# Weight splits ordered behind the scaling of every pair

## The chip, the cores and the metric

The program runs on one core of one Trainium2 chip. The metric is the device time of the whole program in microseconds (us), lower is better; it is given as the median of several executions of the same build.

## What is computed

A two-layer decoder trunk on 256 tokens of width 1024, all in float32, with a memory of 256 tokens beside it. Each layer is half a feed-forward net, a mixer, and another half of a feed-forward net. In the first layer the mixer is a gated short convolution beside a cross-attention to the memory; in the second it is latent attention (MLA), whose shared keys and values come from the residual stream after the first layer, beside another cross-attention.

```python
def swiglu(h, w13, w2):                    # D_FF = 2816
    gate, up = jnp.split(h @ w13, 2, axis=-1)
    return (jax.nn.silu(gate) * up) @ w2

# four times in the trunk (two layers, two halves each):
x = x + 0.5 * swiglu(rms_norm(x, g), w13, w2)
```

## The kernel before

Everything is kept transposed: 128 partitions hold a slice of the model's width, 256 tokens lie along the row. TensorE works on pairs of a high and a low part of each number, so that float32 accuracy survives: a product is two matmuls where one operand is an activation (`mm2`, lines 196 and 197: high weights against 128x512, then low weights against 128x256) and three where both are split (`mm3`, lines 190 to 192).

**Weights.** All weight tiles (128x1024, 512 KB) stand in one list in the order of use, a `Stream` called `W`. SyncE (SP) loads them one after the other into six raw buffers (`wraw`). A tile is *split* into a high part, by a cast on ScalarE (ACT, L69), and a low part, by a subtraction on VectorE (DVE, L70), both into one of eight `whl` buffers. `W.get(key)` hands out the next tile; `W.pump()` issues loads up to 9 tiles and splits up to 5 tiles beyond the last one handed out. While it does so, `issue_after(ins)` for each instruction in `W.hold` puts what it issues behind that instruction in the order of that instruction's engine. The instruction held on is a DVE one, so it is the L70 subtractions that are ordered; casts and loads have no such edge, but a load needs a raw buffer that the subtraction six tiles earlier has freed.

**Stages.** Four half feed-forward stages, with the conv mixer after the first and MLA after the third. A half feed-forward stage goes over 22 *pairs* j = 0 to 21 of a 128-wide slice of gate and one of up. For pair j, `begin(j)` issues 32 matmuls into two PSUM banks (`pg`, `pm`), copies the low half of each bank out on ACT (L483) and adds it to the high half on DVE (L484). `make(j)` scales the result by the row norm R (DVE, L488: the instruction called `evac`), pumps, applies silu (ACT, L494), multiplies gate by up (DVE, L497) and splits the product into the activation tile g (ACT L182, DVE L183). `accumulate` runs two pairs behind and adds g against a tile of w2 (one tile serves two pairs) in 8 matmuls into four banks `acc`. In the first and the third stage some pairs begin with an *insert*, a step of other work: in the first (to about 84 us of the span) the memory's norm and its key and value projections (`spare`, 48 `mm3` matmuls each); in the third (about 504 to 725 us) the shared K/V of MLA: its projection from three tiles at pair 4 (L839 copies it out, L848 to L853 norm it, L860 scales the rotary part), transposes of the latent at pair 6 (L868) and of the rotary part (L881, which waits for the rotary arithmetic on GpSimd, POOL, L800 to L863).

**Order.** A scheduler places the instructions of each engine at build time, by what depends on what and in the order of issue in the text; on the chip each engine then works through its list in that order.

Of the kernel before, what the change touches and what calls it, by code (L numbers as in the profile page):

```python
# [108 lines left out]
def trunk(ctx: ExitStack, tc: tile.TileContext, a, out):  # L109
# [57 lines left out]
    def bank():  # L167
        return pg.tile([P, 2, T], F32, name="pg")

    def mbank():  # L170
        return pm.tile([P, 2, T], F32, name="pm")

    def abank(q):
        return pa.tile([P, 2, T], F32, name=f"acc{q}")

    def keep(i, shape=(P, 2, T), dt=F32R):

        return res.tile(list(shape), dt, name=f"g{i}")
# [10 lines left out]
    def mm3(o, lhs, rhs, start, stop):  # L189
        nc.tensor.matmul(o, lhs[0], rhs[0], start=start, stop=False, skip_group_check=True)  # L190
        nc.tensor.matmul(o, lhs[0], rhs[1], start=False, stop=False, skip_group_check=True)  # L191
        nc.tensor.matmul(o, lhs[1], rhs[0], start=False, stop=stop, skip_group_check=True)  # L192

    def mm2(o, lhs, x, start, stop):

        nc.tensor.matmul(o, lhs[0], x, start=start, stop=False, skip_group_check=True)  # L196
        nc.tensor.matmul(o[:, 0, :], lhs[1], x[:, 0, :], start=False, stop=stop, skip_group_check=True)  # L197
# [54 lines left out]
    W = Stream(tc, wraw, whl, "w", units, 9, 5)  # L252
# [4 lines left out]
    def new_stage():  # L257
        xs["hl"] = res.tile([P, KD, 2, T], F32R, name="xs")
        xs["tot"] = w1.tile([P, T], F32, name="tot")
# [38 lines left out]
    def r_row(s, mk=lambda i: mbank()):  # L298

        rc = xs["rc"] = r_col(s, "x", ps=mk(2))  # L300
        yield
        dg = w1.tile([P, 2, P], F32, name="dg")
        ps = mk(3)
        for t in range(2):
            nc.vector.tensor_scalar(out=dg[:, t, :], in0=ident, scalar1=rc[:, t:t + 1], scalar2=None, op0=ALU.mult)
        for t in range(2):
            nc.tensor.matmul(ps[:, 0, t * P:(t + 1) * P], ones, dg[:, t, :], start=(t == 0), stop=(t == 1),
                             skip_group_check=True)
        R = w1.tile([P, T], F32, name="R")
        nc.vector.tensor_copy(out=R, in_=ps[:, 0, :])  # L310
        yield R


    def evict(d, b, factor, norm):

        xk = xT[:, d, :]
        for h in range(1 if norm is None and d == KD - 1 else 2):
            nc.vector.scalar_tensor_tensor(out=xk, in0=b[:, h, :], scalar=factor, in1=xk, op0=ALU.mult, op1=ALU.add)
        if norm is None:
            nc.sync.dma_start(out=out[:, d * T:(d + 1) * T], in_=xk)  # L320
            return
        if d >= 6:
            feed_square(d)
        feed_split(d, norm)
        if d < 6:
            feed_square(d)

    def accumulate(gen, total_n, bkey, factor, norm):


        acc = [None] * 4
        gs = []
        for n in range(total_n):
            gs.append(gen(n))
            if n % 2 == 0:
                w = W.get(bkey + (n // 2,))
            W.pump()
            for d in range(4):
                if n == 0:
                    acc[d] = abank(d)  # L340
                o = n % 2 * 512 + d * P
                mm2(acc[d], (w[:, 0, o:o + P], w[:, 1, o:o + P]), gs[n], n == 0, n == total_n - 1)
        if norm is not None:
            new_stage()
        for d in range(4):
            evict(d, acc[d], factor, norm)
        for d in range(4, KD):
            b = mbank() if d % 2 else bank()
            for n in range(total_n):
                i, o = divmod((d - 4) * total_n + n, 8)  # L350
                if o == 0:
                    w = W.get(bkey + (total_n // 2 + i,))
                    W.pump()
                ww = (w[:, 0, o * P:(o + 1) * P], w[:, 1, o * P:(o + 1) * P])
                if norm is None and d == KD - 1:
                    mm3(b[:, 0, :], ww, (gs[n][:, 0, :], gs[n][:, 1, :]), n == 0, n == total_n - 1)
                else:
                    mm2(b, ww, gs[n], n == 0, n == total_n - 1)
            evict(d, b, factor, norm)
# [61 lines left out]
    def pairs(keyf, row, bank=bank1, late=False, head=None):  # L421

        st = {}

        def go(n):
            if n == 0 and head is not None:
                st["p0"], st["p1"] = bank(), bank()
                for q in range(4):
                    head(q)
                    c = q // 2  # L430
                    for j in range(2):
                        ps = st[f"p{j}"]
                        w = heads[2 * c + j]
                        for k in (2 * q, 2 * q + 1):
                            for s in range(2):
                                o = k % 4 * 256 + s * P
                                mm2(ps[s], (w[:, 0, o:o + P], w[:, 1, o:o + P]), xs["hl"][:, k], k == 0, k == KD - 1)
                        if q == 3 and j == 0:
                            next(row)
                for c in range(2):  # L440
                    for j in range(2):
                        W.get(keyf(j, c))
                return st["p0"]
            if n == 0:
                st["p0"], st["p1"] = bank(), bank()
                proj(keyf(0, 0), st["p0"], 0)
                proj(keyf(1, 0), st["p1"], 0, lambda: next(row))
                proj(keyf(0, 1), st["p0"], 1)
                if not late:
                    st["R"] = next(row)  # L450
                    proj(keyf(1, 1), st["p1"], 1)
                return st["p0"]
            if n == 1:
                if late:
                    if head is None:
                        proj(keyf(1, 1), st["p1"], 1)
                    st["R"] = next(row)
                return st["p1"]
            ps = bank()
            for c in range(2):  # L460
                proj(keyf(n, c), ps, c)
            return ps
        return go, st

    def rb(R):
        return R.rearrange("p (o t) -> p o t", o=1).broadcast_to([P, 2, T])

    def ffn(l, f, inserts, next_norm, head=None):
        go, st = pairs(lambda j, c: ("w13", l, f, j, c), r_row(xs["tot"], abank), lambda: (bank(), mbank()),
                       True, head)  # L470
        ready = {}
        if head is None:
            with tc.issue_after(xs["fed"][0].ins):
                W.ahead(W.used + 7, W.used + 5)

        def begin(j):
            if j in inserts:
                next(inserts[j], None)
            ps = go(j)
            e = ev.tile([P, 2, T], F32, name="ev")  # L480
            part = wk.tile([P, 2, T], F32, name="sq")
            for s in range(2):
                nc.scalar.copy(out=part[:, s, :], in_=ps[s][:, 1, :])  # L483
                nc.vector.tensor_tensor(out=e[:, s, :], in0=ps[s][:, 0, :], in1=part[:, s, :], op=ALU.add)  # L484
            return e

        def make(j, e):
            evac = nc.vector.tensor_tensor(out=e, in0=e, in1=rb(st["R"]), op=ALU.mult)  # L488
            if j < 2:
                W.hold = (evac.ins,)  # L490
            if j:
                W.pump()
            sl = wk.tile([P, T], F32, name="silu")
            act = nc.scalar.activation(out=sl, in_=e[:, 0, :], func=AF.Silu)  # L494
            xs["evac"], xs["act"] = evac.ins, act.ins
            gg = wk.tile([P, T], F32, name="gg")
            nc.vector.tensor_tensor(out=gg, in0=sl, in1=e[:, 1, :], op=ALU.mult)  # L497
            g = keep(j)
            split(gg, None, g[:, 0, :], g[:, 1, :])
            return g  # L500

        def gen(n):
            if n == 0:
                e0 = begin(0)
                e1 = begin(1)
                ready[0] = make(0, e0)
                ready[1] = make(1, e1)
            if n + 2 < NJ:
                ready[n + 2] = make(n + 2, begin(n + 2))
            return ready.pop(n)  # L510

        accumulate(gen, NJ, ("w2", l, f), 0.5, next_norm)


# [168 lines left out]
    def conv_mixer(next_norm):  # L683
# [60 lines left out]
        def gen(n):  # L744
# [11 lines left out]
            return ready.pop(k)  # L756

        accumulate(gen, 8, ("wo", 0), 1.0, next_norm)


# [550 lines left out]
```

## Time and profile before

| | us |
|---|---|
| median of 3 executions | 977.25 (976.89 to 978.62) |
| the profiled execution, its own time | 978.48 |
| its span in the trace | 976.6 |
| PE busy in the span | 959.2 |
| DVE busy | 741.1 |
| ACT busy | 558.4 |

The span is what the trace covers; the 1.9 us between it and the execution's own time lie around it. "Busy" of PE means that some matmul was in flight. A wait is the time in which an engine stood still, put down to the instruction that released it.

### The profile page before, as it was taken

Reading aid. Unit: us, or ns where it says so; the run is one execution under the profiler, and the core shown is the slowest. Engines: PE = TensorE matmul, PEld = TensorE weight load, DVE = VectorE, ACT = ScalarE, POOL = GpSimd, SP = SyncE. Lnnn points to the kernel's source line nnn. Section 1 sums busy time; section 2 is a strip of 40 time slices with the busy share of each in tenths; the row PEclk is TensorE's granted clock in tenths of the full one; section 3 lists DMA queues with packets and bytes.
Section 4 is the critical chain, followed back from the end, with each engine's and each line's share of the span. In section 5 each row is a group of like instructions: output and inputs, shape, how many; then the busy total and the mean of one; then the engine's idle time right before and its main releaser. Section 6 shows DMA issues by size and latency. Waiting matters only on the chain.

```text
span 976.6 us, 15585 instructions
## 1 busy us (share of the span) xinstructions
PE 959.2 (98%) x5856; PEld 849.7 (87%) x5856; DVE 741.1 (76%) x1412; ACT 558.4 (57%) x961; POOL 22.4 (2%) x47
## 2 busy tenths in 40 slices
PE   8889999999999999999999899999999999999998
PEld 7788898889998888888888788888897998888887
DVE  7978777784988797777858888677778679777771
ACT  7746555554555465555645666556556766555550
POOL 3100000000000000000000200000010000000000
PEclk9989999999999999999999999999999999999999
DMA  8676555551654386666535656554544318756540
GB/s 306 198 249 223 194 186 174 183 197 59 224 187 154 115 281 202 191 199 188 171 117 186 231 175 192 183 194 159 183 139 130 92 45 280 232 194 190 177 133 20
DMA packets 50332, 174.11 MB, mean 178 GB/s; under 512 B 5840, under 2 KB 7376, under 8 KB 50256
## 3 DMA queue, kind: packets, MB, share of 16 engines
q1 hardware_dynamic: 49680, 172.45, 53.4%
q8 instruction: 46, 0.75, 0.3%
q10 hardware_dynamic: 576, 0.66, 0.2%
q14 instruction: 30, 0.25, 0.1%
HBM read 172.04 MB, written 1.05 MB: 177 GB/s over the span
## 4 chain that ended last, share of the span: by engine, by line
PE 91%; DVE 5%; DMA 1%; ACT 1%; issue 1%; POOL 1%; ACTq 0%; POOLq 0%; SPq 0%; DVEq 0%
PE pg L196 20%; PE pm L196 20%; PE pg L197 10%; PE pm L197 10%; PE acc L196 8%; PE acc L197 4%; PE pg L190 2%; PE pg L192 2%; PE pg L191 2%; DVE whl L70 2%; PE pm L190 1%; PE pm L192 1%; PE pm L191 1%; PE acc L190 1%; PE acc L192 1%; PE acc L191 1%
## 5 line engine op out<-in xcount | busy, mean ns | idle before, releaser
L70 DVE TENSOR_TENSOR whl<-wraw,whl 128x1024 fp32r<-128x1024 f32 (+3 forms) x330 | 390.4, 1198 | 94.3 <-ACT whl L69 94.2
L69 ACT CAST whl<-wraw 128x1024 fp32r<-128x1024 f32 (+3 forms) x330 | 338.1, 1029 | 176.2 <-PE pm L197 81.7
L196 PE MATMUL pg<-xs,whl 128*128 128x512 f32 x704 | 255.4, 396 | 1.5 <-ACT whl L69 1.5
L196 PE MATMUL pm<-xs,whl 128*128 128x512 f32 x704 | 254.5, 395 | 0.0
L197 PE MATMUL pg<-xs,whl 128*128 128x256 f32 x704 | 197.4, 280 | 0.8 <-DVE whl L70 0.8
L197 PE MATMUL pm<-xs,whl 128*128 128x256 f32 x704 | 196.3, 279 | 0.0
L196 PEld LDWEIGHTS pg<-xs,whl 128*128 128x128 f32 x704 | 132.1, 188 | 31.5 <-ACT whl L69 2.0
L196 PEld LDWEIGHTS pm<-xs,whl 128*128 128x128 f32 x704 | 132.0, 188 | 30.4 <-ACT g L839 0.2
L196 PE MATMUL acc<-g,whl 128*128 128x512 f32 x384 | 138.8, 397 | 2.6 <-DVE g L183 2.5
L197 PEld LDWEIGHTS pg<-xs,whl 128*128 128x128 f32 x704 | 132.6, 188 | 3.8 <-DVE whl L70 3.6
L197 PEld LDWEIGHTS pm<-xs,whl 128*128 128x128 f32 x704 | 132.6, 188 | 0.3
L197 PE MATMUL acc<-g,whl 128*128 128x256 f32 x384 | 107.1, 279 | 0.0
L196 PEld LDWEIGHTS acc<-g,whl 128*128 128x128 f32 x384 | 72.0, 188 | 21.0 <-DVE g L183 4.5
L197 PEld LDWEIGHTS acc<-g,whl 128*128 128x128 f32 x384 | 72.3, 188 | 0.0
L483 ACT COPY sq<-pm 128x256 f32<-128x256 f32 x88 | 32.8, 372 | 68.8 <-PE pm L197 68.8
L196 PE MATMUL pg<-g,whl 128*128 128x512 f32 x192 | 68.2, 397 | 0.0
L182 ACT CAST g<-gg 128x256 fp32r<-128x256 f32 x94 | 38.0, 404 | 45.4 <-DVE gg L497 41.2
L488 DVE TENSOR_TENSOR ev<-ev,R 128x512 f32<-128x512 f32 x88 | 62.0, 708 | 2.2
L196 PE MATMUL pm<-g,whl 128*128 128x512 f32 x170 | 60.3, 398 | 0.0
L484 DVE TENSOR_TENSOR ev<-pm,sq 128x256 f32<-128x256 f32 x88 | 37.3, 424 | 27.8 <-ACT sq L483 27.7
L183 DVE TENSOR_TENSOR g<-gg,g 128x256 fp32r<-128x256 f32 x94 | 39.7, 422 | 20.6 <-ACT g L182 20.6
L190 PE MATMUL pg<-xs,whl 128*128 128x256 f32 x192 | 55.3, 288 | 0.0
(349 smaller groups left out, 1365.7 us busy)
## 6 DMA issues: line engine op xcount, KB each, us to landing
wraw<-in_w SPq DMA_DIRECT2D x260, 512.0 KB, 4.2
wraw<-in_cin SPq DMA_DIRECT2D x20, 512.0 KB, 4.4
wraw<-in_wo SPq DMA_DIRECT2D x16, 512.0 KB, 3.8
wraw<-in_wmem SPq DMA_DIRECT2D x8, 512.0 KB, 4.7
wraw<-in_qin SPq DMA_DIRECT2D x5, 512.0 KB, 4.3
wraw<-in_mem SPq DMA_DIRECT2D x4, 512.0 KB, 4.6
wraw<-in_wukv SPq DMA_DIRECT2D x4, 384.0 KB, 3.4
wraw<-in_uq SPq DMA_DIRECT2D x4, 384.0 KB, 3.5
```

The source lines that it names most:

```text
L69: nc.scalar.copy(out=h[:, 0, o:o + n], in_=r[:, o:o + n])
L70: nc.vector.tensor_tensor(out=h[:, 1, o:o + n], in0=r[:, o:o + n], in1=h[:, 0, o:o + n].bitcast(F32), op=ALU.subtract)
L182: first = nc.scalar.copy(out=hi, in_=src)
L183: return first, nc.vector.tensor_tensor(out=lo, in0=src, in1=hi.bitcast(F32), op=ALU.subtract)
L190: nc.tensor.matmul(o, lhs[0], rhs[0], start=start, stop=False, skip_group_check=True)
L191: nc.tensor.matmul(o, lhs[0], rhs[1], start=False, stop=False, skip_group_check=True)
L192: nc.tensor.matmul(o, lhs[1], rhs[0], start=False, stop=stop, skip_group_check=True)
L196: nc.tensor.matmul(o, lhs[0], x, start=start, stop=False, skip_group_check=True)
L197: nc.tensor.matmul(o[:, 0, :], lhs[1], x[:, 0, :], start=False, stop=stop, skip_group_check=True)
L483: nc.scalar.copy(out=part[:, s, :], in_=ps[s][:, 1, :])
L484: nc.vector.tensor_tensor(out=e[:, s, :], in0=ps[s][:, 0, :], in1=part[:, s, :], op=ALU.add)
L488: evac = nc.vector.tensor_tensor(out=e, in0=e, in1=rb(st["R"]), op=ALU.mult)
```

## The change

`make` now sets `W.hold` to its `evac` in every pair and not only in pairs 0 and 1, and `accumulate`, which pumped once in each of its steps, now does so only in its last two. So the stream is pumped in `make` of each pair, and the low parts that are issued there stand behind that pair's scaling on DVE. How far loads and splits run ahead, how many there are, and the arithmetic are the same.

```diff
@@ accumulate @@
             gs.append(gen(n))
             if n % 2 == 0:
                 w = W.get(bkey + (n // 2,))
-            W.pump()
+            if n >= total_n - 2:
+                W.pump()
             for d in range(4):
@@ ffn.make @@
             evac = nc.vector.tensor_tensor(out=e, in0=e, in1=rb(st["R"]), op=ALU.mult)
-            if j < 2:
-                W.hold = (evac.ins,)
+            W.hold = (evac.ins,)
             if j:
                 W.pump()
```

From there to `make` the lines stand one lower: L484 is L485 after the change, L488 is L489; from L490 on they agree again. Numbers behind a tile's name are running numbers and differ between the two builds.

How the orders move is shown at three places. First DVE in the first stage, around the scaling of pairs 5 and 6. Before:

```order
L488 TENSOR_TENSOR ev<-ev,R 128x512
L70 TENSOR_TENSOR whl<-wraw,whl 128x1024
L497 TENSOR_TENSOR gg<-silu,ev 128x256
L70 TENSOR_TENSOR whl<-wraw,whl 128x1024 x2
L183 TENSOR_TENSOR g_654<-gg,g_654 128x256
L484 TENSOR_TENSOR ev<-pg,sq 128x256
L70 TENSOR_TENSOR whl<-wraw,whl 128x1024
L484 TENSOR_TENSOR ev<-pm,sq 128x256
L164 TENSOR_SCALAR var_mem<-pm 128x2
L488 TENSOR_TENSOR ev<-ev,R 128x512
```

After the change the same stretch of DVE's list is:

```order
L489 TENSOR_TENSOR ev<-ev,R 128x512
L70 TENSOR_TENSOR whl<-wraw,whl 128x1024 x4
L497 TENSOR_TENSOR gg<-silu,ev 128x256
L485 TENSOR_TENSOR ev<-pg,sq 128x256
L183 TENSOR_TENSOR g_654<-gg,g_654 128x256
L485 TENSOR_TENSOR ev<-pm,sq 128x256
L164 TENSOR_SCALAR var_mem<-pm 128x2
L489 TENSOR_TENSOR ev<-ev,R 128x512
L70 TENSOR_TENSOR whl<-wraw,whl 128x1024 x2
```

Splits that stood between and ahead of the adds of pair 6 (the second and third L484 or L485 on `pg` and `pm`) now stand together, four behind the scaling of pair 5 and two behind that of pair 6, and the adds follow one another with only the split of an activation between them.

Second PE in the first stage, behind the last matmul of pair 7 and at the value projection of the memory. Before, the accumulation of one g stands there, of which these are the last rows, and then the projection begins:

```order
L196 MATMUL acc_433<-g_654,whl 128x512
L197 MATMUL acc_433<-g_654,whl 128x256
L196 MATMUL acc_436<-g_654,whl 128x512
L197 MATMUL acc_436<-g_654,whl 128x256
L190 MATMUL pm<-whl,spare 128x256
L191 MATMUL pm<-whl,spare 128x256
L192 MATMUL pm<-whl,spare 128x256
L190 MATMUL pm<-whl,spare 128x256
```

After:

```order
L196 MATMUL acc_431<-g_654,whl 128x512
L197 MATMUL acc_431<-g_654,whl 128x256
L190 MATMUL pm<-whl,spare 128x256
L196 MATMUL pg<-xs,whl 128x512
L196 MATMUL acc_422<-g_720,whl 128x512
L590 MATMUL pm<-ident,g_825 128x128 x4
L196 MATMUL acc_425<-g_720,whl 128x512
L196 MATMUL acc_428<-g_720,whl 128x512
L196 MATMUL acc_431<-g_720,whl 128x512
L196 MATMUL pg<-xs,whl 128x512
L191 MATMUL pm<-whl,spare 128x256
L192 MATMUL pm<-whl,spare 128x256
```

The next accumulation (g_720) and the transposes L590, which stood behind the projection before, have moved ahead of all but its first matmul; the first high-part matmul of the following pair (`pg`) stands there too.

Third the third stage, behind the shared K/V projection. DVE before:

```order
L186 SCALAR_TENSOR_TENSOR spare<-xT,gc,spare 128x256 x4
L70 TENSOR_TENSOR whl<-wraw,whl 128x1024 x5
L848 TENSOR_TENSOR kv_v<-kv_ms,rk_5630 128x4
L850 TENSOR_SCALAR kv_v<-kv_v 128x4
L152 TENSOR_SCALAR rsy_kv<-kv_v 128x4
L154 TENSOR_SCALAR rsy_kv<-rsy_kv 128x4
L70 TENSOR_TENSOR whl<-wraw,whl 128x1024
L157 SCALAR_TENSOR_TENSOR rst_kv<-rsy_kv 128x4
L70 TENSOR_TENSOR whl<-wraw,whl 128x1024
```

DVE after, with the end of the norm (L853) and what follows it:

```order
L159 SCALAR_TENSOR_TENSOR rsy_kv<-rst_kv,rsy_kv 128x4
L853 TENSOR_TENSOR kv_f<-rsy_kv,rsy_x 128x4
L860 SCALAR_TENSOR_TENSOR g_5729<-g_5700,kv_f,gc 128x64
L860 SCALAR_TENSOR_TENSOR g_5729<-g_5702,kv_f,gc 128x64
L485 TENSOR_TENSOR ev<-pg,sq 128x256
L485 TENSOR_TENSOR ev<-pm,sq 128x256
L489 TENSOR_TENSOR ev<-ev,R 128x512
L70 TENSOR_TENSOR whl<-wraw,whl 128x1024 x5
L497 TENSOR_TENSOR gg<-silu,ev 128x256
```

Before, eight splits stand ahead of and within the norm's chain of small instructions, and the adds and the scaling of pair 4 come behind the chain; after, the splits have gone behind the scaling of pair 4 (L489), and so behind the chain as well. PE there, before (the end of the accumulation behind pair 5):

```order
L197 MATMUL acc_5558<-g_5619,whl 128x256
L196 MATMUL acc_5561<-g_5619,whl 128x512
L197 MATMUL acc_5561<-g_5619,whl 128x256
L868 MATMUL pm<-ident,ev 128x128 x4
L881 MATMUL pm<-ident,g_5730 128x128 x2
L196 MATMUL pg<-xs,whl 128x512
L197 MATMUL pg<-xs,whl 128x256
```

and after (in the middle of the same stretch, behind pair 4):

```order
L197 MATMUL pm<-xs,whl 128x256
L196 MATMUL pm<-xs,whl 128x512
L196 MATMUL pg<-xs,whl 128x512
L868 MATMUL pm<-ident,ev 128x128 x4
L197 MATMUL acc_5547<-g_5544,whl 128x256
L197 MATMUL acc_5550<-g_5544,whl 128x256
L197 MATMUL acc_5553<-g_5544,whl 128x256
L197 MATMUL acc_5556<-g_5544,whl 128x256
L196 MATMUL acc_5547<-g_5619,whl 128x512
L197 MATMUL acc_5547<-g_5619,whl 128x256
```

The transposes L868 now stand earlier, ahead of the second half of the accumulation of g_5544, of all of g_5619 and of nearly all of pair 5. L881 no longer follows them directly: it stands behind pair 5, as before.

## Rows read from the trace of the kernel before

**Rows 1.** The page: busy us, share of the span, instructions, by engine.

```profile
PE 959.2 (98%) x5856; PEld 849.7 (87%) x5856; DVE 741.1 (76%) x1412; ACT 558.4 (57%) x961; POOL 22.4 (2%) x47
```

**Rows 2.** Waits of PE over the span (total us, times, longest us).

```profile
PE pm L881 <- POOL g L863: 2.9, 1, 2.9
PE pm L190 <- DVE ev L484: 2.8, 1, 2.8
PE pg L197 <- DVE whl L70: 0.8, 2, 0.5
PE pm L590 <- DVE g L577: 0.2, 1, 0.2
```

**Rows 3.** Windows (length, busy us and instructions by engine, PEclk, DMA).

```profile
350.00:400.00 50.00, 50.00 (x290) 43.68 (x289) 40.24 (x59) 29.29 (x50) 0.00 (x0) 1.00 0.69 223
57.00:62.40 5.40, 3.20 (x20) 2.59 (x18) 5.40 (x8) 3.28 (x6) 0.00 (x0) 1.00 0.86 303
62.40:69.30 6.90, 6.25 (x29) 6.25 (x30) 4.79 (x19) 1.55 (x3) 0.00 (x0) 0.51 0.82 287
552.00:555.20 3.20, 0.28 (x3) 0.04 (x1) 2.54 (x4) 1.41 (x3) 2.85 (x7) 1.00 0.73 210
555.20:562.00 6.80, 6.80 (x39) 5.96 (x40) 4.46 (x8) 3.86 (x9) 0.00 (x0) 1.00 0.37 126
750.00:775.00 25.00, 24.19 (x166) 21.26 (x165) 18.57 (x62) 20.93 (x59) 0.00 (x0) 0.93 0.26 88
```

**Rows 4.** DVE's timeline before the key projection (start us, busy us).

```profile
58.50 2.36 DVE L70 TENSOR_TENSOR whl<-wraw,whl 128x1024 fp32r<-128x1024 f32 x2
61.44 1.22 DVE L70 TENSOR_TENSOR whl<-wraw,whl 128x1024 fp32r<-128x1024 f32 x1
62.57 0.42 DVE L484 TENSOR_TENSOR ev<-pm,sq 128x256 f32<-128x256 f32 x1
```

**Rows 5.** Windows of PE, tile pm: key, then value projection.

```profile
63.05:71.65 8.60, 8.60 (x48) 0.64 0.59 208
77.98:83.75 5.77, 5.77 (x48) 1.00 0.66 212
```

**Rows 6.** Groups of instructions by line and form (busy us, mean ns; idle before).

```profile
L70 DVE TENSOR_TENSOR whl<-wraw,whl 128x1024 fp32r<-128x1024 f32 x309 | 373.5, 1223 | 89.6 <-ACT whl L69 89.5
L69 ACT CAST whl<-wraw 128x1024 fp32r<-128x1024 f32 x309 | 323.5, 1051 | 162.8 <-PE pm L197 73.5 <-DMA wraw<-in_w 14.6 <-PE pg L197 14.5
L488 DVE TENSOR_TENSOR ev<-ev,R 128x512 f32<-128x512 f32 x88 | 62.0, 708 | 2.2
L483 ACT COPY sq<-pm 128x256 f32<-128x256 f32 x88 | 32.8, 372 | 68.8 <-PE pm L197 68.8
```

**Rows 7.** Timelines of POOL, DVE and PE, 39 to 45 us.

```profile
39.59 1.50 POOL L526 TENSOR_TENSOR g<-g,sq 128x512 f32<-128x512 f32 x1 [0.74 <-ACT sq L525]
39.85 1.78 DVE L488 TENSOR_TENSOR ev<-ev,R 128x512 f32<-128x512 f32 x1
44.89 0.39 PE L197 MATMUL pg<-xs,whl 128*128 128x256 f32 x1
```

**Rows 8.** Timelines of ACT, DVE, POOL and PE around the shared K/V step.

```profile
539.79 0.43 ACT L839 COPY g<-pm 128x320 f32<-128x320 f32 x1 [0.27 <-PE pm L192]
536.99 5.77 DVE L70 TENSOR_TENSOR whl<-wraw,whl 128x1024 fp32r<-128x1024 f32 x5
542.67 0.16 DVE L848 TENSOR_TENSOR kv_v<-kv_ms,rk 128x4 f32<-128x4 f32 x1
548.51 0.48 DVE L860 SCALAR_TENSOR_TENSOR g<-g,kv_f,gc 128x64 f32<-128x64 f32 x2
554.86 0.29 POOL L863 COPY g<-g 128x128 f32<-128x128 f32 x1
543.20 0.40 PE L196 MATMUL acc<-g,whl 128*128 128x512 f32 x1
```

**Rows 9.** The waits of SP's own DMA queue.

```profile
SPq L78 <- DVE whl L70: 427.4, 156, 21.4
```

## The prediction

> **What bounds the kernel.** I read the page first: PE is busy for 959.2 of the span's 976.6 us, DVE for 741.1, ACT for 558.4 [rows 1]. So the time follows PE, and DVE, the only engine whose splits are moved, counts only where PE waits for it. The windows say where that is not: in a steady stretch PE is busy for 50.00 of 50.00 us at full clock, while DVE has 40.24 us of work, that is 10 us of slack [rows 3]. Its 290 matmuls give 0.172 us for one, and so 32 x 0.172 = 5.5 us for a pair and 8 x 0.172 = 1.4 for an accumulation. Then I read PE's waits: 2.8 us of a key-projection matmul (L190) on an add of DVE (L484), 2.9 of a transpose (L881) on POOL, 0.8 in two on splits, 0.2 at the transposes L590 [rows 2]. Last come the windows around the two long waits: behind the first, PE's granted clock is 0.51 for 6.9 us, which is the lower of its two levels, 1.2 GHz; behind the second it stays 1.00 [rows 3].
>
> **What the change removes.** *R1.* In the first stage three splits stand on DVE ahead of the second add of pair 6: two from 58.50, one from 61.44, and the add starts at 62.57 [rows 4], which is when PE is let go. In the new order those splits stand behind the scaling of pair 5 or 6, and the add waits only for its copy. The wait goes: -2.8 us [rows 2]. *R2.* Without that gap there is nothing to drop the clock. The key projection took 8.60 us for 48 matmuls at a mean clock of 0.64, the equal value projection 5.77 at 1.00 [rows 5]: -2.8 us. *R3.* L590 is moved behind other work: -0.2 [rows 2]. *R4.* L881 waits for the copy that ends POOL's rotary chain, at 554.86 + 0.29 [rows 8]. That chain starts from L860 on DVE and keeps its place, while PE reaches L881 later (it must first do pair 5, which will wait, below): 549.9 + 32 x 0.172 = 555.4 us, already 0.3 behind the copy's end, and an accumulation besides. The wait goes: -2.9. Together -8.7 us.
>
> **What it adds in the steady stretches.** In the pairs away from the inserts, the splits issued with a pair (2 or 3 of them, each 1.13 us from start to start [rows 4]) now start when its scaling ends, some 1.5 us after the pair's last matmul (copy 0.37, add 0.42, scaling 0.71 [rows 4, 6]), so the last is done 1.5 + 3 x 1.13 = 4.9 us after it. With five tiles of lead they are the tiles of the pair after next; ahead of it PE has the next pair and two accumulations, 5.5 + 2 x 1.4 = 8.3 us, whose tiles are split already. These matmuls hide the move, with 3.4 us to spare; without that cover each late split would cost its 1.13 us. The product g, behind the splits too, is needed two pairs later. Loads follow the freed raw buffers, as now (SP waits for DVE's splits in 156 places, 427.4 us in all [rows 9]); they come in bunches, but the buffers are held no longer than a pair. I take 0 here and at the stage ends, where pumping goes on as before. Bounds: 0 and, by one late split in each stage, 4 x 1.1.
>
> **What it adds in the first stage.** *A1.* The low part of pair 5's first tile is split behind the scaling of pair 3. At that place DVE runs against POOL: the scaling took 1.78 us instead of 0.71 [rows 6, 7]. From about 38.0: scaling 1.7, two splits of about 1.6, four gain splits 1.7, one split 1.13 make 45.8; PE's matmul with that low part ran at 44.89 [rows 7], +0.9, and the second tile follows with +0.5: 1.4, bounds 0.5 and 2. *A2.* Ahead of the product of pair 5 stand four splits, 4 x 1.13 = 4.5 us; PE needs its g before the key projection, and I get 1.0 from the work that covers it; bounds 0 and 2.3. *A3.* The low part of the first tile for the value projection comes behind the scaling of pair 7: copy, add, scaling and split make 0.37 + 0.35 + 0.61 + 1.13 and hand-overs of 0.2, 2.7 us behind the pair's last matmul. PE has about 2.2 us of other rows there (the second piece of PE's order above), so +0.5, and by the same count +0.45 and +0.35 behind pairs 8 and 10: 1.3, bounds 0 and 2.6. Together +3.7.
>
> **What it adds in the third stage.** *A4.* Pair 4's low part comes behind the scaling of pair 3, which in the trace starts at 532.28 and can start a split earlier, and a split of 640 columns: about 533.4; the rest of the K/V projection covers most: 1.3, bounds 0 and 2.8. *A5.* Before the change eight splits stand ahead of and within the chain of the K/V norm (five from 536.99 [rows 8]), and pair 5 is ready for PE whenever pair 4 is done. Now pair 5's low parts stand behind the scaling of pair 4, which stands behind the chain on DVE. The first copy (L839) starts at 539.79, L848 at 542.67, L860 at 548.51, and pair 4 is done at 543.20, when PE goes on with an accumulation [rows 8]. After the change the low part of the projection's third tile comes behind the scaling of pair 3 too, and I have the projection's end and the first copy near 542.0; ACT's copies and squares take 2.2, 14 small steps at 0.2 us 2.8, and the scaling of the latent (L859) 0.9 with hand-overs, so the transposes can start at about 548.0. PE has done pair 4 at 543.2 + 1.3 and the six high-part matmuls that stand ahead and are ready, 6 x 0.172, at 545.5: +2.5, bounds 0.5 and 3.5. *A6.* PE then does the four transposes L868 and at 548.6 needs the low part of w2, the first split behind the scaling of pair 4. L860, two adds and the scaling take DVE from 547.0 to 548.8, and the split's 1.13 us gives 549.9: +1.3, bounds 0 and 1.5. Together +5.1.
>
> The waits then cancel: -8.7 + 3.7 + 5.1 = +0.1 us in all. *A7.* What is left is the clock. In the third stage PE would stand still for 2.5 + 1.3 = 3.8 us in two pieces with half a microsecond between them. Of the two long gaps of before, 2.8 us with a lower clock behind it and 2.9 without [rows 2, 3], neither settles it; 3.8 is more than either. A second low stretch, 0.93 over 25 us in MLA, cost 0.07 x 25 = 1.75 us [rows 3], the first 2.8 [rows 5]. I take 2.4, nearer the first, for it follows a gap of like kind; bounds 0 and 2.8.
>
> The Trainium skill, "TensorE: Matmul & The Clock Gate" (sections "What's actually happening" and "HAM oscillation"), has the half rate as the state to which a long enough gap without matmuls returns the array. It judges a single gap, not the sum of two; neither of the two pieces that I work out, 2.5 and 1.3 us, is longer than the 2.9 us at 552 that left the clock at 1.00 [rows 2, 3]. By it the clock would stay full here, which is the first rival below; the 0.51 behind 2.8 us of idle [rows 2, 3] speaks against leaning on it.
>
> **Sum.** +0.1 + 2.4 = 2.5 us. The rows are those of an execution of 978.48 us (a span of 976.6 and 1.9 around it), 1.2 above the median; in its terms the sum is 981.0, in those of the median 977.25 + 2.5 = 979.75, which I give as **980.0**, since A1 to A3 are rounded down.
>
> **Rivals.** *The clock stays up* in the third stage: 980.0 - 2.4 = 977.6, no measurable change (a difference below 0.2%, 1.95 us, can't be told from none here). For it speaks the gap at 552 [rows 3], against it the one at 60. *Waits do not form:* only about half of the 8.8 us of new waits appears, because A2, A3 and A6 rest on differences of a few tenths between a chain and its cover, and the three of them together decide it; then the clock stays up too, and R1, R2 and R4 remain: 977.25 - 8.7 + 4.4 = 973, faster. It decides from the point where the new waits stay under 8.7 - 1.95 = 6.75 us. *The first stage drops the clock too:* A2 at its upper bound of 2.3 us behind a piece of A1 puts half clock there again: 980.0 + 2.4 = 982.4. *Nothing happens:* the order shows that splits do move, but if both ends were covered by loads it would be 977.3.
>
> **How the numbers follow.** Forecast 0.35; clock up in the third stage 0.28; waits do not form 0.21; clock down twice 0.11; nothing happens 0.05. So slower 0.46, same 0.33, faster 0.21. The range has to hold most of both neighbours: 974.0 lies between the faster rival and the middle one, 983.5 is the forecast with A1 to A6 nearer their upper bounds, or the double clock drop with a little over. The likeliest case's own range is 978.5 to 982.5.
>
> **What would show it.** R1, R2: PE's wait list has no L190 entry on L485, and the key projection stands at clock 1.00 and 5.8 us. R4: no L881 wait on POOL. A1 to A3: new waits of L197 or L191 on splits (L70) between 44 and 110 us, of 0.3 to 1.4 us each. A5, A6: waits of L868 on L859 and of an L197 of `acc` on L70 near 546 to 550 us, and PEclk at 0.5 behind them for A7. Steady stretches: PE busy for 50.00 of 50.00 us. I am wrong if new waits stand in the second or fourth stage, if the clock stays up everywhere, or if the waits of the first stage come out under 2 us.

## The result and the profile after

The changed kernel takes 986.02 us (984.32 to 987.36, 4 executions) against 977.07 for the kernel before in their company: a ratio of 1.0089, 95% interval 1.0068 to 1.0110, slower by 6.6 to 10.7 us. Timed once more in other company (e9, below) it took 983.08, ratio 1.0071 (1.0049 to 1.0093). The forecast was 980.0 with a range up to 983.5, so the side was right and the size too small: 2.7 us forecast above the median of 977.25, 8.7 and 6.9 measured by these two ratios (9.0 and 4.9 between the medians).

The profiled execution has a span of 985.5 us, 8.9 more than the one of before, and is the longest of the first four. The page has PE with 4.1 us more under matmuls, DVE and ACT with the work they had [rows 1]:

```profile
PE 963.3 (98%) x5856; PEld 848.6 (86%) x5856; DVE 742.6 (75%) x1412; ACT 554.1 (56%) x961; POOL 26.1 (3%) x47
```

Where the time went is told first by one line that comes in the conv mixer and again in MLA, with its first and last start: the kernel before, the profile after, and the changed kernel again in e9.

```profile
L639 ACT ACTIVATE g<-pm,m_nb,mq_rs x16: 554/563/572, 259.9 to 754.1; 128x256 f32<-128x256 f32 x16
L639 ACT ACTIVATE g<-pm,m_nb,mq_rs x16: 553/562/569, 264.6 to 764.5; 128x256 f32<-128x256 f32 x16
L639 ACT ACTIVATE g<-pm,m_nb,mq_rs x16: 552/560/567, 258.6 to 758.7; 128x256 f32<-128x256 f32 x16
```

In the profile after, 4.7 us are lost up to the conv mixer (the first stage), 5.7 more up to MLA (the third), and 1.5 come back after that. In e9, with the same lists, the third stage loses 5.9, but the first reaches the conv mixer 1.3 us earlier than before: the loss there is that of one execution. PE's waits (total, times, longest), to be held against [rows 2]:

```profile
PE pg L197 <- DVE whl L70: 4.3, 6, 1.8
PE acc L196 <- DVE g L183: 3.2, 2, 2.5
PE acc L197 <- DVE whl L70: 2.0, 2, 1.2
PE pg L196 <- DVE ev L485: 1.7, 1, 1.7
PE pm L190 <- DVE ev L485: 1.2, 1, 1.2
PE pm L898 <- DVE ev L485: 1.1, 2, 0.9
PE pm L881 <- DVE ev L485: 0.5, 1, 0.5
PE pm L191 <- DVE whl L70: 0.3, 1, 0.3
```

Of the 3.2 us of `acc` on g, 2.5 are one wait at 27 us that the kernel before has as well:

```profile
PE acc L196 <- DVE g L183: 2.5, 1, 2.5
```

The two long waits of before are gone: no L190 of the first stage waits (the 1.2 us stand in the third), and L881 waits 0.5 us instead of 2.9. In their place are fifteen waits of 0.2 to 1.8 us on low parts (L70) and on what stands behind them. The windows, to be held against [rows 3] and [rows 5] (length, busy us by engine, PEclk, DMA):

```profile
20.00:45.00 25.00, 22.50 (x123) 19.30 (x122) 21.07 (x47) 17.90 (x35) 6.30 (x4) 0.93 0.53 180
64.90:70.90 6.00, 6.00 (x51) 5.96 (x51) 5.18 (x17) 3.77 (x6) 0.00 (x0) 1.00 0.74 274
100.00:125.00 25.00, 23.21 (x127) 19.69 (x126) 19.13 (x30) 14.38 (x23) 0.00 (x0) 0.93 0.62 209
350.00:400.00 50.00, 50.00 (x291) 43.68 (x290) 38.67 (x58) 29.08 (x50) 0.00 (x0) 1.00 0.57 199
550.00:575.00 25.00, 21.59 (x124) 18.07 (x124) 21.01 (x41) 14.71 (x27) 8.25 (x13) 1.00 0.60 193
750.00:775.00 25.00, 23.00 (x158) 19.29 (x157) 22.30 (x69) 19.80 (x53) 0.00 (x0) 1.00 0.37 127
```

The steady stretch is untouched, 50.00 of 50.00. The key projection, now at 64.9 to 70.9 us, runs at full clock. But two windows of the first stage have a mean clock of 0.93, which before had 1.00, while the low stretch in MLA (750 to 775) is not there this time. Each 0.93 over 25 us is about 1.75 us, so the clock cost 3.5 us here and 2.8 + 1.75 = 4.6 before, by this estimate.

The largest new wait shows a chain that the prediction does not have. The timeline of ACT, then DVE, then PE around pair 11 of the first stage (start us, busy us, and in brackets the idle time ahead and what ended it):

```profile
112.73 0.36 ACT L484 COPY sq<-pg 128x256 f32<-128x256 f32 x1
115.37 1.05 ACT L69 CAST whl<-wraw 128x1024 fp32r<-128x1024 f32 x1 [2.27 <-DMA wraw<-in_w]
116.32 0.36 ACT L484 COPY sq<-pm 128x256 f32<-128x256 f32 x1
116.72 0.42 DVE L485 TENSOR_TENSOR ev<-pm,sq 128x256 f32<-128x256 f32 x1 [3.17 <-ACT sq L484]
117.18 0.69 DVE L489 TENSOR_TENSOR ev<-ev,R 128x512 f32<-128x512 f32 x1
117.78 4.63 DVE L70 TENSOR_TENSOR whl<-wraw,whl 128x1024 fp32r<-128x1024 f32 x4
119.06 0.39 PE L197 MATMUL pg<-xs,whl 128*128 128x256 f32 x1 [1.79 <-DVE whl L70]
```

The second copy of the pair stands on ACT behind a cast, and the cast waits 2.27 us for its tile to land. The pair's add, its scaling and the four splits behind the scaling are late by that, and PE stands still for 1.79 us. Before, both copies of this pair stood ahead of the casts:

```profile
110.28 0.37 ACT L483 COPY sq<-pg 128x256 f32<-128x256 f32 x1 [0.41 <-PE pg L197]
111.63 0.37 ACT L483 COPY sq<-pm 128x256 f32<-128x256 f32 x1 [0.98 <-PE pm L197]
111.90 2.21 ACT L69 CAST whl<-wraw 128x1024 fp32r<-128x1024 f32 x2
```

So ACT's list has moved as well as DVE's: by the order of starts in the traces, a cast stands between the two copies in 37 of the 88 pairs, and before in 6. Over the whole span the casts' waits for tiles have grown, before and after:

```profile
ACT whl L69 <- DMA wraw<-in_w: 16.7, 20, 1.9
ACT whl L69 <- DMA wraw<-in_w: 106.9, 117, 4.4
```

### The profile page after: what moved, and what is told of

Its sections match the earlier page's. It is cut to its first block, busy times and chain, and to the rows that moved or that the text cites. A ratio compares the mean times of both kernels' runs of the same rounds, so it can differ in the third digit from the quotient of the medians.

```text
span 985.5 us, 15343 instructions
## 1 busy us (share of the span) xinstructions
PE 963.3 (98%) x5856; PEld 848.6 (86%) x5856; DVE 742.6 (75%) x1412; ACT 554.1 (56%) x961; POOL 26.1 (3%) x47
## 4 chain that ended last, share of the span: by engine, by line
PE 79%; DVE 9%; DMA 6%; ACT 4%; issue 1%; ACTq 0%; SPq 0%; DVEq 0%
PE pg L196 17%; PE pm L196 17%; PE pg L197 9%; PE pm L197 8%; PE acc L196 7%; DVE whl L70 4%; DMA wraw<-in_w 4%; PE acc L197 4%; PE pg L190 2%; PE pg L192 2%; PE pg L191 2%; ACT whl L69 2%; DVE ev L489 1%; PE pm L192 1%; PE pm L191 1%; PE pm L190 1%
## 5 line engine op out<-in xcount | busy, mean ns | idle before, releaser
L69 ACT CAST whl<-wraw 128x1024 fp32r<-128x1024 f32 (+3 forms) x330 | 338.2, 1029 | 212.7 <-DMA wraw<-in_w 106.9
L70 DVE TENSOR_TENSOR whl<-wraw,whl 128x1024 fp32r<-128x1024 f32 (+3 forms) x330 | 383.9, 1203 | 11.8 <-ACT whl L69 11.7
L196 PE MATMUL pg<-xs,whl 128*128 128x512 f32 x704 | 258.1, 398 | 2.3 <-DVE ev L485 1.7
L197 PEld LDWEIGHTS pg<-xs,whl 128*128 128x128 f32 x704 | 133.6, 190 | 10.7 <-DVE whl L70 10.1
L485 DVE TENSOR_TENSOR ev<-pm,sq 128x256 f32<-128x256 f32 x88 | 37.2, 423 | 68.6 <-ACT sq L484 68.5
L489 DVE TENSOR_TENSOR ev<-ev,R 128x512 f32<-128x512 f32 x88 | 61.4, 701 | 2.6
L485 DVE TENSOR_TENSOR ev<-pg,sq 128x256 f32<-128x256 f32 x88 | 37.1, 421 | 27.8 <-ACT sq L484 26.9
L190 PE MATMUL pg<-xs,whl 128*128 128x256 f32 x192 | 55.3, 288 | 0.0
```

The costliest lines, as they stand in the source:

```text
L69: nc.scalar.copy(out=h[:, 0, o:o + n], in_=r[:, o:o + n])
L70: nc.vector.tensor_tensor(out=h[:, 1, o:o + n], in0=r[:, o:o + n], in1=h[:, 0, o:o + n].bitcast(F32), op=ALU.subtract)
```

## The experiments

The changes are short; `NEW` stands for the stages named. They are shown against the changed kernel, those of e6 and e12 against the kernel before, that of e11 against e3. Ratios are to the kernel before, run on the same chip. Where a difference in us is given beside a ratio, it is that of the ratio.

**e1, the hold alone** (the pump in accumulate stays).

```diff
-            if n >= total_n - 2:
-                W.pump()
+            W.pump()
```

> Hold set in every pair, but the pump in accumulate stays. In the build order the engines' lists are those of before but for six places on VectorE. So every theory that puts the loss down to the order expects 977 us, within 2 us of before; one that puts it down to the hold itself, whatever the pumping, expects 984 to 988.

Measured 980.29, ratio 1.0024 (1.0005 to 1.0044): 2.3 us slower. What the expectation says of the lists is wrong: it holds for the other half of the change (e10), and with the hold alone the lists of DVE, PE and ACT move too (by the order of starts in the traces, some 280 of DVE's 1412 rows and 340 of ACT's 961). Casts wait for tiles 55.2 us in 67 cases. So the hold is the half that moves the lists.

**e10, the pump alone** (the hold in the first two pairs, as before).

```diff
-            W.hold = (evac.ins,)
+            if j < 2:
+                W.hold = (evac.ins,)
```

> Pump dropped from accumulate, hold in the first two pairs only. The lists of all engines are those of before but for three places on VectorE where one row moves by one or two: 976 to 979, within 2 us of before. Anything above 981 would say that the build order is not what decides.

Measured 978.51, ratio 1.0005 (0.9988 to 1.0023): nothing. By itself the dropped pump moves three rows of DVE's list and none of PE's or ACT's. With the hold the loss is 4.6 to 6.4 us more than in e1; that this is because one tile in five is then split a pair later fits e8 below, and is not shown by itself.

**e2, e3 and e4, the change in some stages only.**

```diff
-            if n >= total_n - 2:
+            if bkey[1:] not in NEW or n >= total_n - 2:
                 W.pump()
...
-            W.hold = (evac.ins,)
+            if j < 2 or (l, f) in NEW:
+                W.hold = (evac.ins,)
```

> Both edits in the first half feed-forward stage alone, all else as before. The two traces put some 4.7 us of the loss before the conv mixer: 981 to 982 if that is the change's own doing in this stage; 977 to 978 if the half-clock stretches at 31 and 119 us are an accident of one execution and the waits alone cancel. The clock theory also expects that the half-clock stretches do not stand at the same places in this profile.

> Both edits in the third stage alone. The two traces put 5.7 us there: 982 to 983 if the stage is independent of the others; my sum on record without its clock term gives 979.4, and 977 to 978 would say that the loss needs the first stage's late loads carried over.

> Both edits in the second and fourth stage alone, which have no inserts. My sum on record says 0 there: 977 us within 1.5 us. If late loads starve ScalarE's casts everywhere, and the starved casts hold up the copies, 979 to 983.

First stage 979.92, ratio 1.0010 (0.9996 to 1.0024); third stage 982.07, 1.0043 (1.0025 to 1.0061); second and fourth 977.93, 0.9990 (0.9975 to 1.0005). That is +1.0 (-0.4 to +2.3), +4.2 (+2.4 to +6.0) and -1.0 (-2.4 to +0.5) us. In the two stages without inserts the casts wait for tiles as well, and no cost can be measured; the steady stretch stays full. The waits of ACT and two windows of e4:

```profile
ACT whl L69 <- DMA wraw<-in_w: 53.1, 73, 2.0
```

```profile
60.00:70.00 10.00, 7.58 (x59) 7.12 (x58) 8.33 (x23) 3.83 (x6) 0.00 (x0) 1.00 0.81 285
350.00:400.00 50.00, 50.00 (x290) 43.72 (x289) 37.58 (x55) 29.19 (x48) 0.00 (x0) 1.00 0.55 181
```

The first of these windows bears on the clock: the first stage is there as before, L190 waits 2.4 us in it, and the clock stays at 1.00, where it fell to 0.51 in the kernel before [rows 3].

**e11, the third stage without the hold in pairs 3 and 4.**

```diff
-            if j < 2 or (l, f) in NEW:
+            if j < 2 or (l, f) == (1, 0) and j not in (3, 4):
```

> Both edits in the third stage alone, as in e3, but with the hold not renewed in pairs 3 and 4, around the shared K/V projection. If A4 to A6 of my sum are what the third stage loses, the waits at 530, 532, 546 and 549 us go and the time falls from 982 to 977 to 979.5, the wait of L881 coming back with 2.9 us. If the loss lies in late loads over the whole stage, it stays at 981 to 983.

Measured 977.37, ratio 0.9995 (0.9978 to 1.0012): the whole 4.2 us of e3 are gone, and 0.5 more. The mean granted clock is 0.9963 here and 0.9942 in e3, so some 2 of these 4.7 us may be the clock's. PE's waits:

```profile
PE pg L197 <- DVE whl L70: 1.5, 3, 0.8
PE pm L190 <- DVE ev L485: 1.0, 1, 1.0
PE pm L899 <- DVE ev L485: 0.9, 2, 0.6
```

The waits around the shared K/V step, on L485 and on the low part of w2, are not in it, but for a first low part of pair 4 (0.5 us); the L190 in the list is that of the first stage, at 64.7 us. L898 (L899 here) still waits 0.9. L881 did not wait again, unlike what was expected.

**e5 and e6, eight raw and seven split buffers,** in the changed kernel and in the kernel before.

```diff
-    wraw = pool("wraw", 6)
-    whl = pool("whl", 8)
+    wraw = pool("wraw", 8)
+    whl = pool("whl", 7)
```

> The changed kernel with eight raw buffers and seven split buffers instead of six and eight (the same memory). Theory loads: splits that come a pair later free raw buffers late, loads land late, casts that wait for them on ScalarE stand ahead of the copies of the pair, and so the scaling and the next splits are late; two more raw buffers take the wait of casts on loads from 107 us to under 40 and the time to 976 to 981. Theory order: low parts are late because they stand behind the scaling on VectorE, whatever the loads do; 984 to 988.

> The kernel before with eight raw and seven split buffers, the control of the other. Both theories: 975 to 979; what the changed kernel loses against this one, with the same buffers, is 0 to 4 us by theory loads and 7 to 11 us by theory order. More than 980 would say that the seventh split buffer is itself a bound.

The changed kernel takes 975.68 with them, ratio 0.9991 (0.9971 to 1.0011); the kernel before 972.09, ratio 0.9949 (0.9932 to 0.9967). Against the kernel before with the same buffers the changed one loses 3.6 us between the medians, where it lost 4.9 and 9.0 with the old buffers; the change in the loss is hardly more than the noise. In e5 casts wait for tiles ten times less, and of PE's waits the two at the K/V step are what remains, beside six short ones:

```profile
ACT whl L69 <- DMA wraw<-in_w: 11.3, 5, 4.3
```

```profile
PE pg L197 <- DVE whl L70: 2.1, 6, 0.6
PE pg L196 <- DVE ev L485: 1.7, 1, 1.7
PE acc L197 <- DVE whl L70: 1.2, 1, 1.2
```

The build order moves with the buffers too: in e5 a cast stands between the copies in 2 pairs, where the changed kernel had 37. So this does not part what early loads do on the chip from what they do to the lists. e6 is 5.0 us faster than the kernel before; its mean granted clock is 0.9970 against 0.9953, which is 1.7 of the 5. What PE still waits for there, of the waits in [rows 2]:

```profile
PE pm L881 <- POOL g L863: 3.0, 1, 3.0
PE pm L190 <- DVE ev L484: 0.8, 1, 0.8
```

**e12, ten raw and six split buffers,** in the kernel before.

```diff
-    wraw = pool("wraw", 6)
-    whl = pool("whl", 8)
+    wraw = pool("wraw", 10)
+    whl = pool("whl", 6)
```

> The kernel before with ten raw and six split buffers, one step further than e6 (eight and seven). If early loads are what e6 gained by, and they are not yet early enough, 968 to 971; if e6 already has every load in time, 971 to 973; if six split buffers hold back the splits, which go five tiles ahead, 976 to 985.

Measured 972.64, ratio 0.9953 (0.9937 to 0.9969): as e6; casts wait for the tiles of the half feed-forward stages (`in_w`) for 3.6 us in all here and 1.9 in e6, so eight raw buffers already have the tiles in time.

**e7, the casts behind silu too.**

```diff
-            W.hold = (evac.ins,)
-            if j:
-                W.pump()
...
             xs["evac"], xs["act"] = evac.ins, act.ins
+            W.hold = (evac.ins, act.ins)
+            if j:
+                W.pump()
```

> The changed kernel with the casts (ScalarE) of each pump ordered behind silu of the same pair too, so that no cast can stand ahead of that pair's copies. Theory loads: the loop through ScalarE is cut, casts find their tiles loaded, the adds wait less on copies (95 us in the changed kernel) and the time falls to 976 to 982. Theory order: no gain, since the low parts come no earlier; 985 to 990, the high parts being later.

Measured 1004.34, ratio 1.0273 (1.0251 to 1.0295). Casts wait for tiles only 12.2 us, as wanted, but now PE waits for the casts, the high parts:

```profile
PE pg L196 <- ACT whl L69: 8.4, 14, 2.3
PE pg L197 <- DVE whl L70: 6.8, 11, 1.8
PE acc L196 <- ACT whl L69: 4.5, 5, 3.7
PE pm L190 <- ACT whl L69: 3.2, 2, 1.6
```

No cast stands between two copies now, and the kernel is 27 us slower than before. So a cast that waits early on ACT is the lesser evil, and cutting the loop at that end is no cure. It tells the theories apart only in part, for it adds a cost of its own.

**e8, splits six tiles ahead.**

```diff
-    W = Stream(tc, wraw, whl, "w", units, 9, 5)
+    W = Stream(tc, wraw, whl, "w", units, 9, 6)
```

> The changed kernel with splits six tiles ahead instead of five, which gives back the tile that the pump in accumulate used to split a pair earlier. If that one tile's delay is the cause: 975 to 979. If the order behind the scaling is the cause, or if the eight split buffers hold the sixth tile back anyway: 983 to 988.

Measured 977.75, ratio 1.0008 (0.9993 to 1.0023). One tile more of lead gives back nearly all in the time, though some 2 us of it may be the clock's (mean 0.9976 against 0.9953 for the kernel before); casts wait for tiles 38.0 us in 42 cases, and stand between the copies in 10 pairs.

**e9, the changed kernel again.** No edit.

> The changed kernel as it is, in the company of the others. If its loss is a matter of waits, 984 to 988 again, 8 to 10 us over before, and the profile shows the first-stage waits of 1.0 and 0.5 us near 46 and 50 us and the third-stage ones near 535 to 555 us at the same matmuls. The places that hang on a load that lands just in time (2.0 us near 117, 0.9 near 162 us) may be shorter, and the half-clock stretches elsewhere.

Measured 983.08 (981.86 to 986.95, 6 executions). The profile, of an execution with a span of 980.1 us, has the same waits at the K/V step, 1.7 and 1.2 us:

```profile
PE pg L196 <- DVE ev L485: 1.7, 1, 1.7
PE acc L197 <- DVE whl L70: 1.2, 1, 1.2
PE pm L190 <- DVE ev L485: 1.0, 1, 1.0
PE pm L898 <- DVE ev L485: 0.8, 1, 0.8
```

The waits of 0.87 and 0.34 near 46 and 50 us are there with 1.01 and 0.39. Those of 1.79 near 117 and of 0.77 near 162 us are not: 0.34 at the first place, none at the second. Its low clock stands at 8 to 12 us and at 547 to 555, the latter behind the two waits at the K/V step, which end at 546.6 and 548.9.

## Why the prediction was wrong in size

**R1, R3, R4.** L190 and L881 lost their waits as said (2.8, and 2.4 of 2.9); L590 kept its 0.2. (PE is let go in [rows 4] by the end of the add, at 63.0, not by its start.)

**R2 and A7, the clock.** Both are right in kind and too large, and the two errors cancel. In the fourteen traces a low stretch stands at the key projection in three of the four kernels whose L190 waits there for 2.4 us or more (before, e3 and e10, not e4) and in none of the other ten. In the third stage one stands behind the 1.7 + 1.2 us of waiting in e3, e5 and e9, and none in the profile after and in e1 (1.3 + 1.2); but behind the wait of L881, which the change takes away, one stands as often (in e2, e6 and e10, not in before, e4 and e12). So A7 puts one chance in the place of another. Over the executions the mean granted clock is 0.9967 in e2 and 0.9942 in e3, against 0.9951 for the kernel before in their company: about 1.6 us won in the first stage and 0.9 lost in the third (give or take half a microsecond each), where R2 and A7 had 2.8 and 2.4. For the whole change it is 0.9962 (10 executions) against 0.9949 (26, in the company of e9), and 0.0013 x 980 = 1.3 us is in the changed kernel's favour: the clock does not explain the loss.

**Steady stretches, 0.** Right: 50.00 of 50.00, and e4 shows no cost.

**A1 to A6.** The waits that I worked out came, near their places and sizes. First stage, by the idle time in the profile after: A1 0.87 + 0.34 (1.4 said), A2 0.67 (1.0), A3 0.27 + 0.21 (1.3). Third stage: A4 1.20 + 0.65 (1.3), A5 1.70 (2.5), A6 1.20 (1.3). Together 7.1 us of 8.8. The K/V step goes as worked out; DVE and then PE in the profile after, which answer to [rows 8]:

```profile
549.31 0.16 DVE L848 TENSOR_TENSOR kv_v<-kv_ms,rk 128x4 f32<-128x4 f32 x1 [5.67 <-ACT sq L845]
551.90 0.16 DVE L853 TENSOR_TENSOR kv_f<-rsy_kv,rsy_x 128x4 f32<-128x4 f32 x1
552.49 0.42 DVE L485 TENSOR_TENSOR ev<-pg,sq 128x256 f32<-128x256 f32 x1
553.28 0.69 DVE L489 TENSOR_TENSOR ev<-ev,R 128x512 f32<-128x512 f32 x1
553.89 3.65 DVE L70 TENSOR_TENSOR whl<-wraw,whl 128x1024 fp32r<-128x1024 f32 x3
552.97 0.50 PE L196 MATMUL pg<-xs,whl 128*128 128x512 f32 x1 [1.70 <-DVE ev L485]
553.39 0.63 PE L868 MATMUL pm<-ident,ev 128*128 128x128 f32 x4
555.22 0.74 PE L197 MATMUL acc<-g,whl 128*128 128x256 f32 x4 [1.20 <-DVE whl L70]
```

The chain of small steps starts at 549.31 with nothing else for DVE to do (5.67 us idle ahead of it), the adds and the scaling come behind L853, the low parts behind the scaling at 553.89, and PE waits 1.70 and 1.20 us. e11 shows that the hold in pairs 3 and 4 is what the third stage loses by: without it the waits of this step are gone but for 0.5 us, and 4.7 us are won back, some 2 of them perhaps by the clock.

**By stage.** The terms of the sum make 3.7 - 2.8 - 2.8 - 0.2 = -2.1 us for the first stage and 5.1 + 2.4 - 2.9 = +4.6 for the third. Measured were +1.0 (e2) and +4.2 (e3), so what is missed lies in the first stage and in what the whole loses beyond its parts. The third came out in part by luck: A7 was too large, and waits that the sum does not have, at L898 (0.85 and 0.18 us in e3), are in its place.

**The step that failed** is the sentence on the loads: they follow the freed buffers "as now", "the buffers are held no longer than a pair. I take 0". A split held back holds its raw buffer, the load six tiles on starts late, and its cast waits on ACT (16.7 us before, 106.9 after). SP's loads now wait for a split in 299 places, where it was 156 [rows 9]:

```profile
SPq L78 <- DVE whl L70: 763.0, 299, 21.4
```

The middle one of the loads is issued at 462.0 us instead of 444.7, in a kernel that is only some 5 us behind there. With the zero fails the reading that DVE is "the only engine whose splits are moved": ACT's list moved too, and the cast that waits now stands in front of a copy, which is what the next scaling waits for. ACT's idle time ahead of casts that stand between two copies is 0.7 us before, 16.9 after and 13.9 in e9. A pair in the steady stretch has the slack to take it (e4). Around the inserts, of which a second set runs in the first stage to about 139 us, the list of new waits was too short: 0.45, 1.79 and 0.77 us near 58, 117 and 162 us, 0.88, 0.41 and 0.23 at L898 and the pair behind it between 594 and 620 us. That is 4.5 us in the profile after; in e9 it is 1.9 (0.34 and 0.28 near 116 and 134 us, 0.75 and 0.52 at L898). With eight raw buffers nearly all of them go, A2 with them, but so do the casts between the copies (e5): whether the late tile or the moved list weighs more is not shown.

**A second thing that the sum lacks** is a price for a wait beyond its idle time. Two long waits gave way to fifteen, and each costs more than it shows: the matmul behind the wait near 117 us takes 0.39 us where the mean of its kind is 0.28. Taken from start to start of PE's matmuls, against the median step of their kind in the same trace, the 8.9 us between the spans are 4.7 us of idle time in waits of 0.15 us and more (21 of them against 10; 11.6 us of new ones, less 5.2 of the two long ones and 1.7 of short ones in the first 12 us), 3.8 us that these waits cost beyond it, at the wait and in the four matmuls behind, 1.3 us less at the low clock, and 1.7 us elsewhere. In the traces of before, after and e9 the price beyond the idle time is about 0.3 us for one wait; in e9, with 19 waits, it makes 2.5 of the 3.5 us by which its span is longer than that of before.

**The rivals.** Nothing of "waits do not form" was seen, and "the clock stays up" in the third stage came true in the first profile without making the time 977.6.

**What stays open:** why the whole change loses 6.9 to 8.7 us and its parts by stage 4.2 together. The intervals of the parts and of e9 are wide enough to hold one value, that of the first result hardly. The first profile's waits at 117 and 162 us hang on tiles that land just in time; e2, with the same ACT order in the first stage, has 0.3 us and none. So a part of it differs from execution to execution; whether the rest is carried from stage to stage was not tried.

## What to carry to other kernels

An order edge on the instruction that frees a buffer is an edge on the transfer that wants this buffer: follow it through the queue to the instruction that waits for the data, and to what stands behind that one on its engine, whose list may have moved too. Count the waits and not only their idle time: here each cost about 0.3 us beyond it. Slack in the steady stretch says nothing of the places where other work is put in; before a chain that must be done there, the splits for what follows are better placed ahead of it than behind (e11). Where casts wait for loads, moving memory from the second stage of the buffering to the first (here two raw buffers for one of split parts) can be worth more than an order: 5 us of 977, with the change of the lists and of the clock that it brought.

## What the runs showed of the chip

The low clock does not follow from the length of a gap here. Behind 2.9 us of idle at 552 us it stayed at 1.00 before [rows 3]; behind the wait of 2.5 us at 27 us, which every kernel has (2.3 to 2.5), it stayed up before and fell after, and a low stretch follows it in eight of the fourteen traces. The executions of the kernel before differ in mean granted clock from 0.991 to 0.998 and in time from 973 to 982 us; in the company of e9 those at 0.993 and below took 977.75 or more, those at 0.996 973.4 to 976.1.
